# An fp32 encoder trunk on one core: split weights of the up projection 32 bytes off the line of the tokens, and one small load moved in the start

## The chip, the core and the metric

The kernel runs on one core of a Trainium2 chip (trn2). The metric is the device time of one execution in microseconds (us). The kernel before was timed in three runs: 2146.21, 2146.18 and 2145.07 us, median 2146.18. Names used below: TensorE is PE (its weight loads are listed apart as PEld), VectorE is DVE, ScalarE is ACT, GpSimd is POOL; SP only issues transfers (DMAs). SBUF is the on-chip memory of 128 partitions, PSUM the accumulation memory that PE writes.

## The reference

Two layers over 256 tokens of width 2048, everything in float32:

```
for l in range(2):
    h = rms_norm(x, ln1_g[l])
    qa, ka, va, qb, kb, vb = split(h @ w_in[l])           # 2048 -> 4608
    oa = neighborhood_attention(rms_norm(qa), rms_norm(ka), va, rpb[l])
    ob = windowed_gqa_sink(rope(rms_norm(qb)), rope(rms_norm(kb)), vb, sink[l])
    x = x + concat(rms_norm(oa), rms_norm(ob)) @ w_out[l]  # 2048 -> 2048
    h2 = rms_norm(x, ln2_g[l])
    u = depthwise_conv(h2 @ w_up[l], conv_w[l], conv_b[l]) # 2048 -> 11264
    gate, up = u[..., :5632], u[..., 5632:]
    x = x + (silu(gate) * up) @ w_down[l]                  # 5632 -> 2048
```

The weights are read once, 1 MB at a time; nearly all arithmetic is in the four projections.

## The kernel before

**Split products.** A float32 product is made from parts that PE takes at its faster format (float32r). Each operand is cut in two: a high part (ACT copies it rounded, line 103) and a low part (DVE subtracts the high part from the operand, line 104). For weights the parts are the tiles `whi` and `wlo`, 128 x 1024 each, made in `split_w` (lines 586 to 598) from a loaded tile `raw` (128 x 2048, 1 MB, two halves). For tokens the two parts lie side by side in one tile of 2 x 256 columns, called `xs` (the norm's output, 16 tiles, written in `prep_x`) or `mid` (attention's and the gate's outputs). Three of the four partial products are summed: high x high, low token x high weight, high token x low weight.

**Which operand moves.** A matmul has a stationary operand of 128 columns, which a weight load (PEld) brings into the array, and a moving operand that is streamed past it. In the input, output and down projections (`three`, line 387) the tokens are stationary and 512 columns of weights move. In the up projection (`two`, line 382) it is the other way round, so that the result stands transposed for the convolution:

```
mm(ps, w_h, mv, first, False)
mm(ps[:, 1], w_l, mv[:, 0], False, last)
```

The first of the two has a 128-column block of `whi` stationary and both halves of an `xs` tile moving, 512 columns. The second has the same block of `wlo` stationary and the 256 columns of the high half moving. A step of the up projection (half a `raw` tile) is eight such pairs, 16 matmuls; a feature block of 128 gate and 128 up columns is four steps, and there are 44 blocks in each of the two layers: 2 x 44 x 4 x 8 = 2816 pairs.

**The order of the work.** `quanta` (lines 550 to 571) lists the 1 MB pieces in order: 36 of the input projection, 16 of the output projection, and then, chunk by chunk, the up and the down projection. `steps` are their halves. The main loop (line 675) splits the weights four steps ahead (`SPLIT_AHEAD`), so `whi` and `wlo` have five buffers each; loads run three pieces ahead (`LOAD_AHEAD`) on SP's queue.

**Where tiles lie.** The constants come first in each partition of SBUF, then the pool of weights (`raw`, `whi`, `wlo`), then `mid`, `xs` and the rest. The tile `shift` (56 floats, line 73) holds no data and only takes room. In the built program `raw`, all five buffers of `whi` and of `wlo`, all 16 of `xs` and all 16 of `mid` begin 96 bytes past a multiple of 256; `x` begins 128 past one. A 128-column block is 512 bytes of a partition, an `xs` tile 2048, so every block, too, begins 96 past a multiple of 256. A tile `prob_a` of the attention begins 32 past one.

**The start.** ACT issues the load of the norm's weights `ln_g` (line 75) and of the first four pieces of `x` transposed (`mid<-in_xT`, line 605), SP the first 1 MB of weights in four parts, the next ones and the other pieces of `x`. `prep_x` (line 120) needs both a piece and `ln_g`. Eight semaphores, DMAHW0 to DMAHW7, are given to the DMAs in turn; a DMA that gets one in use waits, on its issuing engine, until the DMA before it on that semaphore has landed.

Of the kernel before, what the change touches and what calls it, by code (L numbers as in the profile page):

```python
# [12 lines left out]
F32R = mybir.dt.float32r  # L13
# [5 lines left out]
P = 128  # L19
# [13 lines left out]
FG = 4  # L33
CHUNKS = (12, 12, 12, 8)
# [8 lines left out]
SPLIT_AHEAD = 4  # L43
AHEAD_PRIO = 40
SHIFT = 56
WARM = 14


@with_exitstack
def encoder_kernel(  # L50
# [5 lines left out]
    nc = tc.nc  # L56
    const = ctx.enter_context(tc.tile_pool(name="const", bufs=1))
    wp = ctx.enter_context(tc.tile_pool(name="wp", bufs=2))
# [13 lines left out]

    const.tile([P, SHIFT], F32, name="shift")
    ln_g = const.tile([P, 2, L, KD], F32, name="ln_g")
    nc.scalar.dma_start(out=ln_g, in_=a["ln_g"])
    ident = const.tile([P, P], F32, name="ident")
    make_identity(nc, ident)
    ones = const.tile([P, P], F32, name="ones")
# [297 lines left out]
    quanta = []  # L376
# [28 lines left out]
    def q_win(l, j, u):  # L405
        def body(q, half, hi, lo):
            ps = banks("in", u == 0 and half == 0)
            hv, lv = (w.rearrange("p (k n) -> p k n", k=2) for w in (hi, lo))
            k = 4 * u + 2 * half
            three(ps, (xs[k], xs[k + 1]), hv, lv, k == 0, k == KD - 2)  # L410
            if half == 0:
                return
            if u == 0 and j == 0 and l > 0:
                load_qk_g(l)
            if u == 2 and j == 1:
                rope_tables(l)
            if u == 3:
                if l == 0 and j == 0:
                    at(q + 4, done_win, q, l, j, ps, half=0)
                else:  # L420
                    done_win(q, l, j, ps)
        return body
# [35 lines left out]
    def q_wout(l, grp, nb, u):  # L458
        def body(q, half, hi, lo):
            g = 0 if grp == "a" else 1  # L460
            ps = banks("out", u == 0 and half == 0)
            hv, lv = (w.rearrange("p (k n) -> p k n", k=2) for w in (hi, lo))
            h = 4 * u + 2 * half
            three(ps, (os[g * NH + h], os[g * NH + h + 1]), hv, lv, h == 0, h == NH - 2)
            if nb == 0 and u == 0 and half == 1:
                stat_o(grp)
            if u == 1 and half == 1:
                if grp == "b":
                    add_x(nb, ps, st["ro"])
                else:  # L470
                    whole_x(q, l, 1, nb, ps, st["ro"])
        return body
# [12 lines left out]
    def q_up(l, f, u):  # L485
        def body(q, half, hi, lo):
            if u == 0 and half == 0:
                cur["up"] = psum.tile([P, 2, 2, T], F32, name="mm", bufs=2)
            ps = cur["up"]
            hv, lv = (w.rearrange("p (k j n) -> p k j n", k=4, j=2) for w in (hi, lo))  # L490
            for j in range(2):
                for kk in range(4):
                    k = 8 * u + 4 * half + kk
                    two(ps[:, j], hv[:, kk, j], lv[:, kk, j], xs[k], k == 0, k == KD - 1)
            if u == 1 and half == 1:
                with tc.high_priority(offset=4 * AHEAD_PRIO if f == NF - 1 else 0):
                    glu(l, f, ps)
        return body
# [24 lines left out]
    def q_down(l, c, nb, g):  # L523
        f0, nf = sum(CHUNKS[:c]), CHUNKS[c]

        def body(q, half, hi, lo):
            ps = banks(("dn", nb), g == 0 and half == 0)
            hv, lv = (w.rearrange("p (k n) -> p k n", k=2) for w in (hi, lo))
            i = FG * g + 2 * half
            three(ps, (gs[f0 + i], gs[f0 + i + 1]), hv, lv, i == 0, i == nf - 2,  # L530
                  l == L - 1 and c == len(CHUNKS) - 1 and i == nf - 2)
            if g < nf // FG - 1 or half == 0:
                return
            if c < len(CHUNKS) - 1:
                add_x(nb, ps)
            elif l + 1 < L:
                whole_x(q, l + 1, 0, nb, ps)
            else:

                n = 2 if nb == NB - 1 else 1  # L540
                for tt in range(TT):
                    for i in range(n):
                        m = slice(i * 512 // n, (i + 1) * 512 // n)
                        xv = x[:, tt, nb * 512 + m.start:nb * 512 + m.stop]
                        nc.vector.tensor_add(xv, xv, ps[:, tt, m])  # L545
                        (nc.sync, nc.scalar)[i].dma_start(
                            out=out[:, tt, nb * 512 + m.start:nb * 512 + m.stop], in_=xv)
        return body

    for l in range(L):  # L550
        for j in range(NJ):
            for u in range(4):
                quanta.append((a["w_in"][l, j, u], q_win(l, j, u)))
        for grp in "ba":
            for nb in range(NB):
                for u in range(2):
                    quanta.append((a["w_out"][l, 0 if grp == "a" else 1, nb, u], q_wout(l, grp, nb, u)))
        f = 0
        for c, nf in enumerate(CHUNKS):

            end = min(sum(CHUNKS[:c + 1]) + 1, NF)
            while f < end:
                for u in range(2):
                    quanta.append((a["w_up"][l, f, u], q_up(l, f, u)))
                f += 1
            ng = nf // FG
            order = [(nb, g) for nb in range(NB) for g in range(ng)]
            if end == NF:
                order = sorted(order, key=lambda o: (o[0] // 2, o[1], o[0]) if o[0] < 2 else (1, 0, 0))
            for nb, g in order:  # L570
                quanta.append((a["w_down"][l, sum(CHUNKS[:c]) // FG + g, nb], q_down(l, c, nb, g)))


    steps = [(q, h) for q in range(len(quanta)) for h in range(2)]
# [1 line left out]
    raw, hl, left, loads, highs = {}, {}, {}, {}, {}  # L576
# [9 lines left out]
    def split_w(s, parts=1):  # L586
        if s < len(steps):
            q, half = steps[s]
            hl[s] = tuple(wp.tile([P, 1024], F32R, name=t, bufs=SPLIT_AHEAD + 1) for t in ("whi", "wlo"))
            m = 1024 // parts  # L590
            for j in range(parts):
                with tc.high_priority(offset=AHEAD_PRIO if s >= KD // 2 else 0):
                    highs[s] = split(*(t[:, j * m:(j + 1) * m] for t in hl[s]),
                                     raw[q][:, half * 1024 + j * m:half * 1024 + (j + 1) * m])
            left[q] -= 1
            if left[q] == 0:
                del raw[q]
                load(q + LOAD_AHEAD)
# [3 lines left out]
    for i in range(KD // 2):  # L602
        xT.append(act.tile([P, 2, T], F32, name="mid", bufs=16))
        if i < 4:
            nc.scalar.dma_start(out=xT[i], in_=a["xT"][:, 2 * i:2 * i + 2, :])
        if i == 1:

            nc.scalar.activation(const.tile([P, 1], F32, name="junk"), halfpi, AF.Copy)
# [156 lines left out]
```

## Time and profile before

| | us |
|---|---|
| median of three runs | 2146.18 |
| the profiled execution's own time | 2145.43 |
| its span, first to last instruction | 2143.6 |
| PE busy | 2135.3 |
| DVE busy | 1460.9 |
| ACT busy | 1141.2 |
| POOL busy | 66.5 |

The profile is of one execution. Its own time is 1.8 us longer than its span and 0.75 us shorter than the median. The granted clock of PE was 1.000 throughout, its upper level of 2.4 GHz. Matmuls are pipelined: the duration in a row is from the issue of one to the modelled end of its last column, so it is longer than the distance from one matmul's start to the next one's. The distances between starts are what adds up to the span.

### The profile page before, as it was taken

How to read it: one execution, taken by the hardware profiler on the slowest of the kernel's cores; microseconds unless marked ns; L12 is line 12 of the kernel's file. 1: busy time of each engine (PE TensorE's matmuls, PEld its weight loads, DVE VectorE, ACT ScalarE, POOL GpSimd, SP SyncE). 2: the span in 40 equal slices, each digit the busy share in tenths (PEclk: the TensorE clock that was granted, in tenths of full speed). 3: DMA queues.
4: the chain of work that ended last, by engine and by line, in shares of the span. 5: the costliest groups of instructions: out<-in, count | busy, mean ns of one | idle time of the engine just before them, and what ended most of it. 6: DMA issues, size and time to landing. Idle time of an engine off the chain costs nothing.

```text
span 2143.6 us, 28802 instructions
## 1 busy us (share of the span) xinstructions
PE 2135.3 (100%) x10904; PEld 1811.6 (85%) x10904; DVE 1460.9 (68%) x2293; ACT 1141.2 (53%) x1651; POOL 66.5 (3%) x215
## 2 busy tenths in 40 slices
PE   9999999999999999999999999999999999999999
PEld 7888888888888888888888888888888888888887
DVE  7777667775677567657756866677756775776575
ACT  6566556554455355535655665555545553554453
POOL 0000000000000000000000000000000000000000
PEclk9999999999999999999999999999999999999999
DMA  9544555555555555555555454555555555555553
GB/s 340 195 142 166 175 177 177 188 186 197 183 190 191 190 189 179 194 196 178 195 179 194 138 170 164 177 177 185 189 197 180 193 188 188 194 179 194 193 181 137
DMA packets 60844, 397.89 MB, mean 186 GB/s; under 512 B 7329, under 2 KB 9889, under 8 KB 13729
## 3 DMA queue, kind: packets, MB, share of 16 engines
q1 hardware_dynamic: 59696, 394.71, 54.0%
q8 instruction: 85, 1.39, 0.3%
q10 hardware_dynamic: 1008, 1.34, 0.2%
q14 instruction: 55, 0.44, 0.1%
HBM read 393.93 MB, written 2.10 MB: 185 GB/s over the span
## 4 chain that ended last, share of the span: by engine, by line
PE 99%; DMA 1%; ACT 0%; DVE 0%; issue 0%; DVEq 0%
PE mm L85 95%; PE pv L85 1%; PE S L85 1%; PE tr L291 1%; PE S L139 0%; DMA raw<-in_w_in 0%; PE tr L352 0%; PE tr L85 0%; ACT xs L106 0%; DMA ln_g<-in_ln_g 0%; ACT whi L103 0%; PE tr L347 0%; PE tr L344 0%; DVE x L545 0%; DVEq L760 0%
## 5 line engine op out<-in xcount | busy, mean ns | idle before, releaser
L104 DVE TENSOR_TENSOR wlo<-raw,whi 128x1024 fp32r<-128x1024 f32 (+1 forms) x737 | 901.2, 1223 | 560.0 <-ACT whi L103 520.4
L103 ACT ACTIVATE whi<-raw 128x1024 fp32r<-128x1024 f32 (+1 forms) x737 | 779.7, 1059 | 882.0 <-PE mm L85 680.2
L85 PE MATMUL mm<-xs,whi 128*128 128x512 f32 x2816 | 995.0, 399 | 0.0
L85 PE MATMUL mm<-xs,wlo 128*128 128x256 f32 x2816 | 790.9, 281 | 0.0
L85 PEld LDWEIGHTS mm<-xs,whi 128*128 128x128 f32 x2816 | 528.8, 188 | 131.3
L85 PEld LDWEIGHTS mm<-xs,wlo 128*128 128x128 f32 x2816 | 531.9, 189 | 0.7
L85 PE MATMUL mm<-whi,mid 128*128 128x512 f32 x1920 | 481.6, 391 | 0.0
L85 PEld LDWEIGHTS mm<-whi,mid 128*128 128x128 f32 x1920 | 357.9, 188 | 72.8
L85 PE MATMUL mm<-whi,xs 128*128 128x512 f32 x1152 | 296.1, 395 | 2.8 <-ACT whi L103 2.7
L85 PE MATMUL mm<-wlo,mid 128*128 128x512 f32 x960 | 260.0, 390 | 0.0
L85 PEld LDWEIGHTS mm<-whi,xs 128*128 128x128 f32 x1152 | 214.6, 188 | 47.4 <-ACT whi L103 3.4
L85 PEld LDWEIGHTS mm<-wlo,mid 128*128 128x128 f32 x960 | 180.1, 188 | 37.3
L85 PE MATMUL mm<-wlo,xs 128*128 128x512 f32 x576 | 162.0, 396 | 0.0
L516 DVE SCALAR_TENSOR_TENSOR pT<-halo,conv,pT 128x256 f32<-128x256 f32 x352 | 146.3, 474 | 0.2
L85 PEld LDWEIGHTS mm<-wlo,xs 128*128 128x128 f32 x576 | 107.3, 188 | 21.7 <-DVE wlo L104 0.4
L514 ACT ACTIVATE pT<-halo,conv 128x256 f32<-128x256 f32 x176 | 94.9, 587 | 0.1
L508 POOL COPY halo<-halo 128x6 f32<-128x6 f32 x88 | 18.5, 210 | 1453.9 <-DVE halo L506 1453.9
L506 DVE TENSOR_TENSOR halo<-prob,r 128x512 f32<-128x512 f32 x88 | 60.9, 692 | 2.7
L505 DVE TENSOR_TENSOR prob<-prob,mm 128x512 f32<-128x512 f32 x88 | 59.8, 680 | 0.0
L452 DVE TENSOR_TENSOR x<-x,mm 128x1024 f32<-128x1024 f32 x28 | 34.2, 1221 | 35.2 <-PE mm L85 35.2
L504 ACT ACTIVATE prob<-mm 128x512 f32<-128x512 f32 x88 | 51.0, 580 | 0.0
L519 DVE TENSOR_TENSOR prob<-prob,pT 128x256 f32<-128x256 f32 x88 | 36.8, 418 | 1.5 <-ACT prob L518 1.5
(129 smaller groups left out, 841.1 us busy)
## 6 DMA issues: line engine op xcount, KB each, us to landing
raw<-in_w_up SPq DMA_DIRECT2D x176, 1024.0 KB, 4.8
raw<-in_w_down SPq DMA_DIRECT2D x88, 1024.0 KB, 4.9
raw<-in_w_in SPq DMA_DIRECT2D x71, 1024.0 KB, 4.9
raw<-in_w_out SPq DMA_DIRECT2D x32, 1024.0 KB, 4.9
bias<-in_bias SPq DMA_DIRECT2D x16, 160.0 KB, 3.7
x<-in_x SPq DMA_DIRECT2D x4, 512.0 KB, 8.3
out<-x SPq DMA_DIRECT2D x6, 256.0 KB, 2.7
raw<-in_w_in SPq DMA_DIRECT2D x4, 256.0 KB, 5.7
```

The source lines that it names most:

```text
L85: nc.tensor.matmul(ps, lhsT, rhs, start=start, stop=stop, skip_group_check=True)
L103: high = nc.scalar.activation(hi, src, AF.Copy)
L104: nc.vector.tensor_sub(lo, src, hi.bitcast(F32))
L291: nc.tensor.transpose(ps[:, j, tt * P:(tt + 1) * P], qn[tt][:, p + j, :], ident)
L452: nc.vector.tensor_add(xv, xv, ps)
L504: nc.scalar.activation(t, ps[:, :, 0], AF.Copy)
L505: nc.vector.tensor_add(t, t, ps[:, :, 1])
L506: nc.vector.tensor_mul(ux[:, :, r:r + T], t, st["r2"][:, None, :].to_broadcast([P, 2, T]))
L508: nc.gpsimd.tensor_copy(ux[:, :, 1:r], ux[:, :, T:T + r - 1])
L514: nc.scalar.activation(y[:, j, :], ux[:, j, r:r + T], AF.Identity, scale=w1, bias=b)
L516: nc.vector.scalar_tensor_tensor(y[:, j, :], ux[:, j, o:o + T], w, y[:, j, :], op0=ALU.mult, op1=ALU.add)
L519: nc.vector.tensor_mul(t[:, 1, :], t[:, 0, :], y[:, 1, :])
```

## The change

There are two parts. First, `whi` and `wlo` get 64 floats (256 bytes) more per buffer, and a step of the up projection uses the 1024 columns from float 56 on, the others those from float 0 on. In the built program a step of the up projection then finds its split weights 64 bytes past a multiple of 256, that is 32 below its tokens (`xs`, still 96), and the other projections theirs at 96 as before. The buffers grow by 256 bytes each, so all that lies behind them moves up by 2560 bytes and keeps its place within 256. Second, the load of `ln_g` is issued behind that of the first piece of `x` and no longer ahead of it.

```
+UP_AT = 56
...
     ln_g = const.tile([P, 2, L, KD], F32, name="ln_g")
-    nc.scalar.dma_start(out=ln_g, in_=a["ln_g"])
...
-                    quanta.append((a["w_up"][l, f, u], q_up(l, f, u)))
+                    quanta.append((a["w_up"][l, f, u], q_up(l, f, u), True))
...
-            hl[s] = tuple(wp.tile([P, 1024], F32R, name=t, bufs=SPLIT_AHEAD + 1) for t in ("whi", "wlo"))
+            at_ = UP_AT if quanta[q][2] else 0
+            hl[s] = tuple(wp.tile([P, 1024 + 64], F32R, name=t, bufs=SPLIT_AHEAD + 1)[:, at_:at_ + 1024]
+                          for t in ("whi", "wlo"))
...
         if i < 4:
             nc.scalar.dma_start(out=xT[i], in_=a["xT"][:, 2 * i:2 * i + 2, :])
+        if i == 0:
+            nc.scalar.dma_start(out=ln_g, in_=a["ln_g"])
```

The pieces of the other three projections get `False` in the same place. The order of instructions on PE, DVE, POOL and SP is the same in both programs. It differs on ACT, at the head of its program; `mid_83` and `mid_82` below are the same first piece of `x`, `raw_97` the first 1 MB of weights, `xs0` and `xs1` the first two token tiles. Before:

```order
L75 DMA ln_g_72<-in_ln_g 128x64
L605 DMA mid_83<-in_xT 128x512
L605 DMA mid_85<-in_xT 128x512
L608 ACT_TABLE_LOAD
L608 ACTIVATE junk_87<-halfpi_81 128x1 [waits DVE_49]
L605 DMA mid_89<-in_xT 128x512
L605 DMA mid_91<-in_xT 128x512 [waits DMAHW1_49]
L106 ACTIVATE xs0_135<-mid_83,ln_g_72 128x256 [waits DMAHW3_49,DMAHW0_49]
L106 ACTIVATE xs1_138<-mid_83,ln_g_72 128x256
L103 ACTIVATE whi_141<-raw_97 128x512 [waits DMAHW2_49]
L103 ACTIVATE whi_141<-raw_97 128x512
```

The same head of ACT's program in the changed kernel:

```order
L608 DMA mid_82<-in_xT 128x512
L610 DMA ln_g_72<-in_ln_g 128x64
L608 DMA mid_85<-in_xT 128x512
L613 ACT_TABLE_LOAD
L613 ACTIVATE junk_87<-halfpi_80 128x1 [waits DVE_49]
L608 DMA mid_89<-in_xT 128x512
L608 DMA mid_91<-in_xT 128x512 [waits DMAHW1_49]
L107 ACTIVATE xs0_135<-mid_82,ln_g_72 128x256 [waits DMAHW3_49,DMAHW0_49]
L107 ACTIVATE xs1_138<-mid_82,ln_g_72 128x256
L104 ACTIVATE whi_141<-raw_97 128x512
L104 ACTIVATE whi_141<-raw_97 128x512 [waits DMAHW2_49]
```

The first two loads have changed places, and with them their semaphores: DMAHW0 was `ln_g`'s and is now the first piece's, DMAHW3 the other way round. The second 1 MB of weights, fifth DMA on SP, waits for DMAHW0 in both programs: before for the landing of `ln_g`, now for that of the first piece of `x`. The wait for DMAHW2 (the second quarter of the first weights) moved from the first to the second of the two halves of the first split.

## Rows read from the trace of the kernel before

**Rows 1.** The page's head, the busy time of PE, the granted clock of PE in 40 equal slices, and the chain of work that ended last, by engine and by line.

```profile
span 2143.6 us, 28802 instructions
...
PE 2135.3 (100%) x10904; PEld 1811.6 (85%) x10904; DVE 1460.9 (68%) x2293; ACT 1141.2 (53%) x1651; POOL 66.5 (3%) x215
...
PEclk9999999999999999999999999999999999999999
...
PE 99%; DMA 1%; ACT 0%; DVE 0%; issue 0%; DVEq 0%
```

**Rows 2.** The page's costliest groups: line, engine, operation, tiles and shapes, count, then busy us and mean ns of one, then idle us of the engine before them and what ended it.

```profile
L104 DVE TENSOR_TENSOR wlo<-raw,whi 128x1024 fp32r<-128x1024 f32 (+1 forms) x737 | 901.2, 1223 | 560.0 <-ACT whi L103 520.4
L103 ACT ACTIVATE whi<-raw 128x1024 fp32r<-128x1024 f32 (+1 forms) x737 | 779.7, 1059 | 882.0 <-PE mm L85 680.2
L85 PE MATMUL mm<-xs,whi 128*128 128x512 f32 x2816 | 995.0, 399 | 0.0
L85 PE MATMUL mm<-xs,wlo 128*128 128x256 f32 x2816 | 790.9, 281 | 0.0
...
L85 PEld LDWEIGHTS mm<-xs,wlo 128*128 128x128 f32 x2816 | 531.9, 189 | 0.7
```

**Rows 3.** PE's timeline from 405 us on, inside the up projection of the first layer: start us, duration us, engine, line, operation, tiles, shape, count. 98 pairs lie between the first row's start and the last row's.

```profile
404.77 0.40 PE L85 MATMUL mm<-xs,whi 128*128 128x512 f32 x1
405.00 0.28 PE L85 MATMUL mm<-xs,wlo 128*128 128x256 f32 x1
405.12 0.40 PE L85 MATMUL mm<-xs,whi 128*128 128x512 f32 x1
405.35 0.28 PE L85 MATMUL mm<-xs,wlo 128*128 128x256 f32 x1
405.47 0.40 PE L85 MATMUL mm<-xs,whi 128*128 128x512 f32 x1
405.71 0.28 PE L85 MATMUL mm<-xs,wlo 128*128 128x256 f32 x1
405.83 0.40 PE L85 MATMUL mm<-xs,whi 128*128 128x512 f32 x1
...
439.39 0.40 PE L85 MATMUL mm<-xs,whi 128*128 128x512 f32 x1
```

**Rows 4.** PE's timeline from 485 us on, inside the down projection of the first layer; rows of the same tiles are merged with their count, the first number is the start of the first.

```profile
487.06 1.07 PE L85 MATMUL mm<-wlo,mid 128*128 128x512 f32 x4
487.96 1.98 PE L85 MATMUL mm<-whi,mid 128*128 128x512 f32 x8
489.78 1.07 PE L85 MATMUL mm<-wlo,mid 128*128 128x512 f32 x4
```

**Rows 5.** PE's timeline from 340 us on, at the very beginning of the up projection of the first layer. Nine pairs lie between the first row's start and the last row's.

```profile
340.48 0.39 PE L85 MATMUL mm<-xs,whi 128*128 128x512 f32 x1
340.71 0.28 PE L85 MATMUL mm<-xs,wlo 128*128 128x256 f32 x1
340.82 0.39 PE L85 MATMUL mm<-xs,whi 128*128 128x512 f32 x1
...
343.60 0.39 PE L85 MATMUL mm<-xs,whi 128*128 128x512 f32 x1
```

**Rows 6.** PE's timeline at two places where a 512-column matmul of the projections is followed by a transpose of the attention, whose stationary block begins elsewhere within 256 bytes. The weight load (PEld) of the transpose begins with the matmul ahead of it.

```profile
224.43 0.14 PEld L344 LDWEIGHTS tr<-ident,prob_a 128*128 128x128 f32 x1
224.67 0.27 PE L344 MATMUL tr<-ident,prob_a 128*128 128x128 f32 x1
...
147.24 0.39 PE L85 MATMUL mm<-wlo,xs 128*128 128x512 f32 x1
147.47 0.38 PE L352 MATMUL tr<-ident,prob 128*128 128x128 f32 x2
```

**Rows 7.** Busy us of each engine, with counts, in a stretch inside the up projection (us from the span's start), then the granted clock, the DMA share and GB/s. The columns are PE, PEld, DVE, ACT, POOL.

```profile
360.00:480.00 120.00, 120.00 (x681) 104.09 (x680) 90.98 (x131) 67.05 (x97) 6.42 (x22) 1.00 0.55 189
```

**Rows 8.** The chain that ended last, in order of time, over the first 25 us: start us, us, what.

```profile
0.73 3.68 DMA ln_g<-in_ln_g
...
4.43 8.43 DMA raw<-in_w_in
...
12.88 2.01 ACT whi L103 x2
14.89 3.27 ACT xs L106 x9
...
19.89 2.11 PE mm L85 x8
```

**Rows 9.** The timeline of the start: the two DMA issues on ACT's queue, ACT's first token tile with the idle time before it, and PE's first matmul of a projection.

```profile
0.73 0.41 ACTq L75 DMA_DIRECT2D ln_g<-in_ln_g  x1
...
1.17 0.94 ACTq L605 DMA_DIRECT2D mid<-in_xT  x2
...
6.60 0.91 ACT L106 ACTIVATE xs<-mid,ln_g 128x256 fp32r<-128x256 f32 x2 [2.96 <-DMA mid<-in_xT]
...
8.54 0.91 ACT L106 ACTIVATE xs<-mid,ln_g 128x256 fp32r<-128x256 f32 x2
```

**Rows 10.** The page's DMA issues: what, queue, count, KB each, median us from issue to landing.

```profile
raw<-in_w_in SPq DMA_DIRECT2D x71, 1024.0 KB, 4.9
```

More of the change, by code (lines that the diff above doesn't have):

```diff
@@ L552, in encoder_kernel @@
             for u in range(4):
-                quanta.append((a["w_in"][l, j, u], q_win(l, j, u)))
+                quanta.append((a["w_in"][l, j, u], q_win(l, j, u), False))
         for grp in "ba":
@@ L556, in encoder_kernel @@
                 for u in range(2):
-                    quanta.append((a["w_out"][l, 0 if grp == "a" else 1, nb, u], q_wout(l, grp, nb, u)))
+                    quanta.append((a["w_out"][l, 0 if grp == "a" else 1, nb, u], q_wout(l, grp, nb, u), False))
         f = 0
@@ L570, in encoder_kernel @@
             for nb, g in order:
-                quanta.append((a["w_down"][l, sum(CHUNKS[:c]) // FG + g, nb], q_down(l, c, nb, g)))
+                quanta.append((a["w_down"][l, sum(CHUNKS[:c]) // FG + g, nb], q_down(l, c, nb, g), False))
     steps = [(q, h) for q in range(len(quanta)) for h in range(2)]
```

## The prediction

> **What bounds the kernel now.** I read the page's head and its chain first: PE is busy for 2135.3 of 2143.6 us, the chain that ended last is 99% PE, and the clock stands at its upper level in every slice [rows 1]. So the time is the sum of the distances from one matmul's start to the next, and an edit counts by what it does to those distances. Then the groups: the up projection is 2816 pairs of a 512-column and a 256-column matmul, each with a weight load of its own, and PE stood idle before none of them [rows 2]. DVE and ACT, which split the weights, were idle for 560 and 882 us before their splits, ACT mostly because it waited for PE to free a buffer [rows 2]; in 120 us of the up projection they are busy for 91 and 67 us [rows 7]. They follow PE and do not set the pace.
>
> The durations of rows 2 can't be used for the price, as they overlap. The timeline gives the distances. In the up projection 98 pairs take from 404.77 to 439.39 us, 34.62 us, or 353.3 ns a pair [rows 3]. Times 2816 that is 995 us, 46% of the execution. In the down projection twelve matmuls of 512 columns take from 487.06 to 489.78, or 226.7 ns each [rows 4]. If the 512-column matmul of the up projection took no more, the other one would be left with 126.6 ns; the rows show 0.23 to 0.24 us for the first and 0.12 for the second [rows 3]. So the same 512 columns cost some 10 ns more here than there, though both have one weight load beside them and both read blocks that lie alike within 256 bytes.
>
> One more thing in the timeline decides what I forecast. The distances are not constant in time. Deep in the up projection the 512-column matmul alternates between 0.23 and 0.24 us [rows 3]; at its beginning, with the same tiles and the same shapes, nine pairs take from 340.48 to 343.60, 3.12 us, or 346.7 ns each, steadily [rows 5]. Nothing waited in either stretch. The same work thus has two paces, and what differs can only be how the two streams that PE reads, the moving columns and the next stationary block, lie to each other in time. The part of the change that counts shifts just that: where the one stream begins in memory beside the other.
>
> **The change part by part.**
>
> *Offset of the split weights.* It adds no instruction and no wait. Per pair both weight loads now read from 32 bytes below the line of the moving tokens. The trace before has no load at that offset in this projection, so its cost is bounded from both sides:
>
> - From below by the shortest distance of either matmul that the rows show with a load beside it: 226.7 ns [rows 4] and 0.11 us (340.71 to 340.82) [rows 5], together 337 ns. That is 16.3 ns less than now, times 2816: 46 us off.
> - From above by the longest pair in the rows, 405.47 to 405.83, 0.36 us, taken by every pair and not by one in three [rows 3]: 6.7 ns more, times 2816: 19 us on top. A farther end: the load of a transpose's block that lies 64 bytes below the line of the moving weights. From its start to the transpose is 224.43 to 224.67, 0.24 us [rows 6], where a load in line takes 226.7 ns [rows 4]; 13 ns more on each 512-column matmul would be 37 us on top. With the block 96 bytes above the line it was 0.23 (147.24 to 147.47) [rows 6].
>
> I take the value that the same work has already shown, the steady pace at the beginning of the up projection: 353.3 - 346.7 = 6.6 ns a pair, times 2816 pairs = 18.6 us off. It is nearest to the rows (same tiles, same shapes, same loads), and it lies between the two ends.
>
> The Trainium skill speaks against any effect: SBUF — State Buffer, section "Who interferes with whom", gives PE two read ports, one for the moving operand and one for weight loads, which are independent of each other. By that rule the offset changes nothing and the sum is zero. The trace doesn't bear it out as it stands: two paces for the same work [rows 3, 5] are hard to explain without some dependence between the two streams. The page TensorE: Matmul & The Clock Gate, section "Back-to-back issue gap", gives N / 2.4 + 2.5 ns for a lone matmul, an estimate of 216 + 109 = 325 ns a pair, which would be 80 us off; no row here shows so short a pair.
>
> *Writes to the shifted tiles.* In 352 steps (2816 pairs, eight to a step) one write of ACT and one of DVE go 32 bytes elsewhere. ACT takes 1059 ns and DVE 1223 for one [rows 2], and a step of eight pairs lasts 2.83 us. Even if each took a fifth longer, DVE's share in rows 7 would rise from 91 to about 102 of 120 us. Cost nothing; the cover is the idle time of both engines. The larger buffers add no wait.
>
> *The load of `ln_g` behind the first piece of `x`.* The start is bound by transfers: PE's steady work begins at 19.89 us, behind ACT's splits, which run without a pause from 12.88, when the second 1 MB of weights has landed [rows 8]. That load was issued at 4.43, the moment `ln_g` had landed. Now it waits for the first piece of `x`. This one was issued at 1.17 and ACT began to use it at 6.60, 5.4 us later [rows 9]; issued at 0.73 it would land about 6.1. So the weights' load goes out some 1.7 us later, and behind it on SP's queue wait the other pieces of `x`. The load took 8.43 us [rows 8], where one of the same size takes 4.9 later on [rows 10]: 3.5 us of it were spent behind transfers issued earlier. A start 1.7 us later fits into that, as the same bytes are ahead of it. I cost it at nothing, with the ends -0.4 us (the first piece comes 0.44 us sooner, and all follows) and +1.7 us (nothing is absorbed). The first matmuls may start 0.4 us sooner, but ACT's next tile already stands at 8.54 behind the first ones [rows 9], and all of them meet again at the landing at 12.85.
>
> **Sum.** The profiled execution took 2145.4 us. 2145.4 - 18.6 + 0 = 2126.8. The median of the runs is 0.75 us above the profiled execution: 2127.6, which I round to 2127.
>
> **The rivals.**
>
> 1. *The offset does nothing.* The two streams don't depend on the offset, and the two paces have another cause, such as the moment at which a stretch begins. For it: the profile names no wait, and all blocks of rows 3 and 5 lie alike, so within the rows it is not the address that makes the difference. Against it: so far no other cause is in sight. Time 2146, give or take the 1.7 us of the start. The rule of the skill's SBUF page would give this time.
> 2. *Slower: the offset moves every load into the worse of the places that the streams can have.* The pairs of rows 3 change between 0.35 and 0.36 us; the alternation shows that a part of them meets a better place by itself, as each pair's length moves the next. A fixed offset can hold all of them at the bad one: +19 us, 2165; with the 13 ns of rows 6 on each 512-column matmul 2183. It decides as soon as the mean pair is above 353.3 ns. For it: a block 64 bytes below the line gave the longest distance of rows 6, and 32 bytes below lies between that and the line. Against it: that was a transpose's load, which is another kind of instruction (0.14 us against 0.19).
> 3. *Faster by much more:* both matmuls reach their shortest distances, 337 ns a pair, 46 us off, 2100. For it: the down projection holds 226.7 ns over its whole length [rows 4]. Against it: in the up projection no pair does.
>
> **How the numbers follow.** Forecast, a pair near 347 ns, with the cases around it down to 340: 0.50. Rival 3: 0.08. Rival 1: 0.18. Rival 2: 0.24. A measurement of this kernel can tell a difference of about 0.2%, 4.3 us, from none. Faster by more than that: 0.50 + 0.08 = 0.58. Within it: 0.18. Slower: 0.24. The likeliest case's own range is 2106 to 2139 us (pairs of 339 to 351 ns). The range for 8 in 10 reaches from 2100, the lower bound, to 2162: it takes in rival 1 and about half of rival 2, and leaves out some 0.05 below and 0.13 above.
>
> **What would show it.** In the profile after, the starts in PE's timeline inside the up projection: 98 pairs in 34.0 us or less if I am right, 34.6 for rival 1, 35 or more for rival 2, 33.0 for rival 3. The pace should be steady and no longer alternate. The distances in the input, output and down projections should stay at 226.7 ns. In the start, the second weights' load should be issued near 6.1 us and still land within 0.5 us of 12.85; if PE's steady work begins past 21, that step is wrong. The forecast as a whole is wrong if the mean pair stays above 351 ns.

## The result and the profile after

| | before | after |
|---|---|---|
| median of the runs beside each other, us | 2145.62 (2144.95 to 2146.21, four runs) | 2126.09 (2125.99 to 2126.18, four runs) |
| ratio | | 0.9909, 95% interval 0.9892 to 0.9926 |
| the profiled execution's own time, us | 2145.43 | 2126.1 |

The changed kernel is 0.9% faster, about 19.5 us. The forecast was 2127, its range 2100 to 2162.

The head of the page after, with the busy time, the granted clock in 40 slices and the chain that ended last, answers to [rows 1]:

```profile
span 2124.3 us, 28802 instructions
...
PE 2118.1 (100%) x10904; PEld 1815.3 (85%) x10904; DVE 1458.0 (69%) x2293; ACT 1141.2 (54%) x1651; POOL 142.1 (7%) x215
...
PEclk9999999999999999999999999999999999999999
...
PE 99%; DMA 0%; ACT 0%; DVE 0%; ACTq 0%; DVEq 0%; issue 0%
```

The number of instructions is the same, PE is still the bound and the clock at its upper level. The whole gain is in PE's busy time, 2135.3 to 2118.1, and the 2 us around it. POOL's busy time doubled, which nobody asked for; the last section comes back to it.

The costliest groups after (busy us, mean ns of one, idle us of the engine before them) answer to [rows 2]. Lines 104 to 107 of the changed kernel are lines 103 to 106 of the one before, line 86 was 85:

```profile
L86 PE MATMUL mm<-xs,whi 128*128 128x512 f32 x2816 | 976.6, 390 | 0.0
L105 DVE TENSOR_TENSOR wlo<-raw,whi 128x1024 fp32r<-128x1024 f32 (+1 forms) x737 | 901.2, 1223 | 543.8 <-ACT whi L104 504.9
...
L86 PE MATMUL mm<-xs,wlo 128*128 128x256 f32 x2816 | 794.1, 282 | 0.0
```

The 512-column matmul of the up projection became 9 ns shorter (399 to 390), the 256-column one did not. These durations overlap, so the price is read from the starts. PE's timeline from 405 us on (start us, duration us) answers to [rows 3]:

```profile
404.82 0.39 PE L86 MATMUL mm<-xs,whi 128*128 128x512 f32 x1
405.05 0.28 PE L86 MATMUL mm<-xs,wlo 128*128 128x256 f32 x1
405.17 0.39 PE L86 MATMUL mm<-xs,whi 128*128 128x512 f32 x1
405.39 0.28 PE L86 MATMUL mm<-xs,wlo 128*128 128x256 f32 x1
405.51 0.39 PE L86 MATMUL mm<-xs,whi 128*128 128x512 f32 x1
...
438.79 0.39 PE L86 MATMUL mm<-xs,whi 128*128 128x512 f32 x1
```

Between the first and the last row lie 98 pairs, as in [rows 3], in 33.97 us: 346.6 ns a pair, where it was 34.62 us and 353.3. A pair is now always 0.34 or 0.35 us and no longer 0.35 and 0.36. In the trace as a whole the pairs away from other work average 346.67 ns. The down projection beside it (timeline from 484 us on, rows of the same tiles merged, answers to [rows 4]):

```profile
484.45 1.98 PE L86 MATMUL mm<-whi,mid 128*128 128x512 f32 x8
486.27 1.07 PE L86 MATMUL mm<-wlo,mid 128*128 128x512 f32 x4
487.17 1.98 PE L86 MATMUL mm<-whi,mid 128*128 128x512 f32 x8
```

Twelve matmuls in 487.17 - 484.45 = 2.72 us, 226.7 ns each, as before. So (353.3 - 346.67) x 2816 = 18.7 us of the difference between the two profiled executions, 19.3 us, come from the pace of the up projection. The rest is the start. Its chain in order of time (start us, us, what) answers to [rows 8]:

```profile
1.17 5.02 DMA ln_g<-in_ln_g
...
6.28 0.91 ACT xs L107 x2
7.19 0.53 ACT whi L104
...
7.76 0.50 PE mm L86
...
8.28 12.82 PE mm L86 x55
```

And the timeline of the start, by ACT and by SP's queue, answers to [rows 9]:

```profile
6.28 0.91 ACT L107 ACTIVATE xs<-mid,ln_g 128x256 fp32r<-128x256 f32 x2 [2.64 <-DMA ln_g<-in_ln_g]
...
11.98 2.01 ACT L104 ACTIVATE whi<-raw 128x1024 fp32r<-128x1024 f32 x2 [1.21 <-DMA raw<-in_w_in]
```

```profile
0.73 4.41 SPq L585 DMA_DIRECT2D raw<-in_w_in  x5
```

Before, PE's first matmul of a projection, which the text of [rows 9] names and its rows don't show, was this one:

```profile
8.59 2.11 PE L85 MATMUL mm<-whi,xs 128*128 128x512 f32 x8 [2.69 <-ACT whi L103]
```

Now `ln_g`, issued second, is what ACT waits for, the first projection matmul starts at 7.76 instead of 8.59, and the second 1 MB of weights has landed at 11.98, not 12.88. The fifth issue of SP's row is that load; the row ends at 0.73 + 4.41 = 5.14 us.

### The profile page after: what moved, and what is told of

It is laid out like the page before. It is cut to its first block, busy times and chain, and to the rows that moved or that the text cites. A ratio compares the mean times of both kernels' runs of the same rounds, so it can differ in the third digit from the quotient of the medians.

```text
span 2124.3 us, 28802 instructions
## 1 busy us (share of the span) xinstructions
PE 2118.1 (100%) x10904; PEld 1815.3 (85%) x10904; DVE 1458.0 (69%) x2293; ACT 1141.2 (54%) x1651; POOL 142.1 (7%) x215
## 4 chain that ended last, share of the span: by engine, by line
PE 99%; DMA 0%; ACT 0%; DVE 0%; ACTq 0%; DVEq 0%; issue 0%
PE mm L86 95%; PE pv L86 1%; PE S L86 1%; PE tr L292 1%; PE S L140 0%; PE tr L353 0%; PE tr L86 0%; DMA ln_g<-in_ln_g 0%; PE tr L348 0%; PE tr L345 0%; DVE x L546 0%; ACT xs L107 0%; ACT whi L104 0%; ACTq L608 0%; DVEq L765 0%
## 5 line engine op out<-in xcount | busy, mean ns | idle before, releaser
L105 DVE TENSOR_TENSOR wlo<-raw,whi 128x1024 fp32r<-128x1024 f32 (+1 forms) x737 | 901.2, 1223 | 543.8 <-ACT whi L104 504.9
L86 PE MATMUL mm<-xs,whi 128*128 128x512 f32 x2816 | 976.6, 390 | 0.0
L509 POOL COPY halo<-halo 128x6 f32<-128x6 f32 x88 | 22.7, 258 | 1359.8 <-DVE halo L507 1359.8
L510 POOL COPY halo<-halo 128x6 f32<-128x6 f32 x88 | 95.1, 1081 | 0.2 <-POOL halo L509 0.2
```

What stands on the lines that cost most here:

```text
L86: nc.tensor.matmul(ps, lhsT, rhs, start=start, stop=stop, skip_group_check=True)
L105: nc.vector.tensor_sub(lo, src, hi.bitcast(F32))
L509: nc.gpsimd.tensor_copy(ux[:, :, 1:r], ux[:, :, T:T + r - 1])
L510: nc.gpsimd.tensor_copy(ux[:, :, T + r:T + 2 * r - 1], ux[:, :, r + 1:2 * r])
```

## The experiments

The theory: the time of a pair depends on where the stationary blocks begin beside the moving tokens, modulo 256 bytes, and on nothing else of the change. Offsets below are given as weights minus tokens, modulo 256; the change is 224. A pace is the mean distance from the start of one high-part matmul to the next in the trace; where a block of 32 pairs has an offset of its own, its first 14 pairs are left out. The first block of each layer has matmuls of other work between its pairs, and its pace is less certain.

**One part at a time.** The changed kernel with `ln_g` loaded first again (offset alone), and with `UP_AT = 0` (the moved load and the larger buffers alone):

```
+    nc.scalar.dma_start(out=ln_g, in_=a["ln_g"])
...
-        if i == 0:
-            nc.scalar.dma_start(out=ln_g, in_=a["ln_g"])
```

> The changed kernel with the load of the norm's weights back in its old place, ahead of the first piece of x: only the offset of 32 bytes in the up projection is left. Theory A (the offset makes the whole pace of the up projection, 346.7 ns a pair): about 18.4 us below the kernel before, near 2127, and PE's first matmul of a projection again near 8.6 us. If the 0.9 us that the start of the changed kernel gained came from a chance of that run and not from the moved load, the start may come out either way here.

> The changed kernel with an offset of 0: the larger weight buffers and the moved load stay. Theory A: the up projection is back at 353.3 ns a pair, so the time is within 1 us of the kernel before, some 0.9 us below it if the moved load is what brought the start forward (first projection matmul near 7.8 us, second weights landed near 12.0), and equal if not. Rival (the larger buffers, not the offset, changed the pace): about 18 us below.

| | us | ratio to before |
|---|---|---|
| offset alone | 2126.50 (5 runs) | 0.9915 (0.9902 to 0.9929) |
| moved load and larger buffers alone | 2144.77 (11 runs) | 0.9998 (0.9990 to 1.0007) |
| before, beside both | 2144.93 (15 runs) | |

The offset is the change. The moved load is worth nothing that these timed runs can tell. The second kernel also bears out that offsets count modulo 256: its split weights lie in buffers an odd multiple of 256 bytes apart, and its pairs took 353.2 ns on average, as before. The groups of the second kernel have the up projection back at the durations of [rows 2]:

```profile
L86 PE MATMUL mm<-xs,whi 128*128 128x512 f32 x2816 | 995.0, 399 | 0.0
```

**Other offsets.** One kernel gives each five feature blocks of the up projection another offset; one does so with the input and down projections, whose tokens are stationary and whose weights move (the output projection stays in line there).

```
-                    quanta.append((a["w_up"][l, f, u], q_up(l, f, u), True))
+                    quanta.append((a["w_up"][l, f, u], q_up(l, f, u), UP_STEPS[l][f // 5]))
...
-            at_ = UP_AT if quanta[q][2] else 0
+            at_ = quanta[q][2]
```

> The changed kernel with the offset of the up projection's weights set anew for every five feature blocks: in the first layer 0, 32, 64, 96, 128, 160, 192, 224 bytes and 0 again, in the second 16, 48, 80, 112, 144, 176, 208, 240 and 224. Theory A (the offset between the two streams sets the pace): each offset has a pace of its own, 353.3 ns a pair at 0 both times, 346.7 at 224 bytes. Rival (either pace can hold at any offset, by how a stretch begins): 353.3 and 346.7 turn up without order, and the two stretches at 0, or the stretch at 224, differ from the whole kernels. I expect paces between 340 and 365.

> The changed kernel, up projection as it is, with the moving weights of the input projection (one offset per job) and of the down projection (one per five pieces) set to the same series of offsets. In line these matmuls take 226.7 ns each. Theory A: the distance changes with the offset here too, and in line need not be the best; I expect 220 to 240 ns. If it stays at 226.7 at all offsets, the dependence is one of the up projection alone.

The mean distances by offset; those of the down projection, where no other work lies between the matmuls, by the offset of its stationary tokens from the moving weights:

```
offset, bytes      0          16    32    48    64    80    96   112   128   144   160   176   192   208   224         240
up pair, ns    353.0       346.9 353.3 346.7 353.2 353.2 346.7 353.3 351.1 349.3 350.0 349.3 353.3 349.9 346.7 346.7/353.3
down mm, ns    226.7 226.7/236.5 233.3 234.7 233.4 233.3 234.2 233.3 233.2 226.7 233.3 231.2 229.0 233.3 233.4       231.8
```

The first took 2136.78 us, the second 2143.91, one run each. Two numbers stand where stretches at one offset differ: the up projection at 240 held 346.7 ns in the two blocks ahead of a stretch of the down projection and 353.3 in the three behind it; the down projection at 16 took 236.5 in one piece and 226.7 in the four of the next stretch. So the theory's "each offset has a pace of its own" already fails at these places. Each kind of matmul has its own list of good offsets: nothing is better than in line for the down projection (144 equals it), and in line is among the worst for the up projection, where 16, 48, 96 and 224 reach 346.7 to 346.9. Nothing grows steadily with the distance: for the up projection 32 bytes above the tokens (32) is no better than in line, 32 below (224) is among the best. In the input projection, in the two jobs of each layer that no other work disturbs, the matmuls took, by the same offset of tokens from weights, 233.4 ns at 224, 233.3 at 208, 229.0 at 192 and 231.2 at 176, as in the down projection.

**Offset or address.** The kernel before with its up projection's tokens moved up by 32 bytes, the weights where they were; and with `SHIFT` 48 for 56, so that everything lies 32 bytes lower and stays in line.

```
-        xs[k] = act.tile([P, 2, T], F32R, name=f"xs{k}")
+        at_ = XS_AT if which == 1 else 0
+        xs[k] = act.tile([P, 2 * T + 64], F32R, name=f"xs{k}")[:, at_:at_ + 2 * T].rearrange("p (j t) -> p j t", j=2)
```

> The kernel before, with the split tokens of the up projection moved up by 32 bytes (128 past a multiple of 256) and the weights left at 96: again the weights begin 32 below the tokens, but at their old address. Theory A (the offset between the two streams counts): 346.7 ns a pair, about 18 us below the kernel before. Rival B (the address of the weights counts, 64 past a multiple of 256): 353.3 ns and the time of before.

> The kernel before, with the placeholder tile 32 bytes shorter, so that weights and tokens all begin at 64 past a multiple of 256, still in line. Theory A: nothing changes, 353.3 ns a pair and the time of before. Rival B (the address of the weights counts): 346.7 ns and about 18 us below.

Tokens moved: 2127.31 us (two runs), ratio 0.9917 (0.9888 to 0.9945). All moved: 2145.87 (eight runs), ratio 1.0001 (0.9990 to 1.0013). The weights' address is the old one in the first, and the weights' address is the change's in the second. So it is the relative offset that counts. Past the first block of the up projection ACT and DVE write `whi` and `wlo` and read `raw`, while `xs` is read by PE alone; that moving `xs` by itself gives the pace of the change shows that the two operands of PE count, and not how its weights lie to the tiles of other engines.

**Two paces at one offset.** Before each feature block but the first a small extra matmul, of 16 to 128 columns, shifts the moment at which the block is entered; layer 0 has offset 0, layer 1 has 224.

```
+                if f:
+                    kick = psum.tile([P, T], F32, name="pv", bufs=1)
+                    mm(kick[:, 0:16 * (f % 8) + 16], ones, ones[:, 0:16 * (f % 8) + 16], True, True)
```

> The changed kernel with offset 0 in the first layer and 32 below in the second, and ahead of each feature block but the first of a layer one small extra matmul of 16 to 128 columns whose result is not used, to throw the matmuls out of step. Theory A in its strict form (the offset alone sets the pace): the first layer's blocks fall back to 353.3 ns a pair within some ten pairs, the second layer's to 346.7. Theory C (at offset 0 both paces can hold, and the way a stretch begins decides, as at the beginning of the up projection in the kernel before): some blocks of the first layer run at 346.7 to their end, others at 353.3; in the second all run at 346.7.

It took 2153.07 us, with 86 matmuls more. At offset 224 every block ran at 346.6 to 346.7 ns. At offset 0 eight of the 43 blocks behind an extra matmul (2, 6, 10, 16, 22, 30, 34 and 40) held 346.5 ns to their end, the other 35 ran at 352.9 to 353.6. PE's timeline in blocks 1 and 2, 18 pairs from the first row to the last in each fence:

```profile
350.87 0.40 PE L86 MATMUL mm<-xs,whi 128*128 128x512 f32 x1
...
357.23 0.40 PE L86 MATMUL mm<-xs,whi 128*128 128x512 f32 x1
```

```profile
362.33 0.40 PE L86 MATMUL mm<-xs,whi 128*128 128x512 f32 x1
...
368.57 0.40 PE L86 MATMUL mm<-xs,whi 128*128 128x512 f32 x1
```

6.36 and 6.24 us, 353.3 and 346.7 ns a pair: the same tiles, shapes and offset, in neighbouring blocks. An offset can thus hold more than one pace, as Theory C had it; the strict form of Theory A is wrong. Between such blocks nothing differs but how they are entered. What in the entry decides was not found: the width of the extra matmul alone doesn't, as 48 columns led to 346.5 ns in blocks 2, 10 and 34 and to 353.5 in 18, 26 and 42. What [rows 3] and [rows 5] showed side by side is this.

**Finer steps.** The up projection's weights in steps of 4 bytes, a block each, and the same for each 1 MB piece of the down projection.

```
+                    quanta.append((a["w_up"][l, f, u], q_up(l, f, u), (NF * l + f) % 64))
```

> The changed kernel with another offset of the up projection's weights for each feature block, in steps of 4 bytes: 0 to 252 bytes, and from the 65th block on 0 to 92 again. Theory A: the pace is a function of the offset, the blocks with the same offset agree, and 353.3 ns at 0 and 346.7 at 224 come out as in the whole kernels. I expect that no offset goes below 346 ns; one that does would be a better kernel.

> The up projection keeps its offset; in the down projection each 1 MB piece has its own offset of the split weights from the tokens, 0 to 252 bytes in steps of 4. Theory (a pair or a lone matmul has a floor that depends only on which streams run side by side, and an offset can only reach it or miss it): no offset of the down projection is below 226.7 ns a matmul, several reach it, others lie up to 10 ns above; mean about 231, that is 1408 x 2 x 4.5 ns = some 10 to 15 us over the changed kernel, near 2138. Rival (the floor of 226.7 is the price of one place, a finer offset gives less): at some offsets a distance of 224 ns or less.

The up projection (2136.77 us, one run): 16 of the 64 offsets (16, 24, 44, 48, 84, 96, 152, 164, 180, 184, 196, 204, 224, 232, 240 and 244) reach 346.4 to 346.8 in every block that has them; 0 and 8 did so in one of their two blocks. Of the 24 offsets that occur twice, 0, 8 and 20 differ by more than 1 ns between their blocks (at 20 it is 353.7 and 350.1); the others agree. No offset is below 346. Two are far above the rest: 156 with 361.6 and 60 with 364.2 and 364.4. PE's timeline at 60 bytes:

```profile
572.64 0.39 PE L85 MATMUL mm<-xs,whi 128*128 128x512 f32 x1
572.87 0.28 PE L85 MATMUL mm<-xs,wlo 128*128 128x256 f32 x1
572.99 0.40 PE L85 MATMUL mm<-xs,whi 128*128 128x512 f32 x1
573.23 0.28 PE L85 MATMUL mm<-xs,wlo 128*128 128x256 f32 x1
573.34 0.42 PE L85 MATMUL mm<-xs,whi 128*128 128x512 f32 x1
573.60 0.29 PE L85 MATMUL mm<-xs,wlo 128*128 128x256 f32 x1
573.74 0.39 PE L85 MATMUL mm<-xs,whi 128*128 128x512 f32 x1
...
579.20 0.39 PE L85 MATMUL mm<-xs,whi 128*128 128x512 f32 x1
```

Here the pairs take 0.35, 0.35 and 0.40 us in turn, 18 of them 6.56 us. The same work over all 2816 pairs would be (364.3 - 353.3) x 2816 = 31 us slower than before; that whole kernel wasn't run. The down projection (2140.09 us, one run; offsets again as stationary minus moving, here tokens minus weights) found no offset below the 226.7 ns of in line; the next best was 228.4 at 196, the worst some 240 at 60, 156, 188 and 236. At 144, which had held 226.7 in the coarse sweep, it was some 231 here: two paces again. The theory's floor held; that several offsets reach it did not, as only in line did. Its time came near for a wrong reason: it counted 2816 matmuls at some 231 ns, where the down projection has 2112 (1056 in each layer) and they averaged some 233.5. 2112 x 6.8 ns is 14 us, and the run was 14.0 us above the changed kernel.

**Two offsets.** The high and the low part get offsets of their own, all 64 combinations of multiples of 32 bytes, a block each.

```
-            hl[s] = tuple(wp.tile([P, 1024 + 64], F32R, name=t, bufs=SPLIT_AHEAD + 1)[:, at_:at_ + 1024]
-                          for t in ("whi", "wlo"))
+            at_ = quanta[q][2]
+            hl[s] = tuple(wp.tile([P, 1024 + 64], F32R, name=t, bufs=SPLIT_AHEAD + 1)[:, o:o + 1024]
+                          for t, o in (("whi", at_ % 64), ("wlo", at_ // 64)))
```

> The high and the low split weights of the up projection get offsets of their own, all 64 combinations of multiples of 32 bytes, a block each. Theory (each weight load meets the moving stream of the matmul it lies beside, so each of the two has an offset of its own that counts): pairs between 346.7 and 356 ns, the good ones 346.7, with the price of the high and of the low part adding up; none below 346.7. Rival (only one of the two loads matters): the pace follows the one offset and is the same for all values of the other. Rival (346.7 is no floor): a combination near 342 or less, which would make a faster kernel than the changed one.

It took 2134.54 us. The pace in ns by the offset of the high part (across) and of the low part (down); the first 24 combinations occur in both layers, with two numbers where they differ by over 0.3. The first number at 0 and 0 and the one at high 128, low 160 are from the disturbed first blocks of the layers:

```
low\high      0           32          64          96          128    160    192         224
  0     349.7/353.3     351.3   349.9/353.1 346.8/349.9     352.1  349.3  340.2/350.1 344.4/346.7
 32        346.7        353.4      351.1       343.5        352.1  349.4     346.6       348.8
 64        346.8     351.3/348.4   353.2       348.4        346.7  348.9     346.7       346.7
 96        346.6        353.3      353.4       346.7        351.8  353.3     348.9       346.6
128        346.7        353.2      350.1       351.2        351.4  346.6     346.6       348.9
160        350.9        350.7      353.3       353.4        351.1  350.0     349.2       353.3
192        351.2        351.2      353.3       353.3        353.3  353.6     353.4       353.3
224        353.0        346.5      350.9       346.8        346.7  346.6     349.0       346.7
```

Both offsets count, so the rival by which only one load matters falls; but they don't add up, which the theory had said: the high part at 32 for 0 costs 6.7 ns with the low part at 96 and nothing with it at 160 or 192. And 346.7 is no floor. High 192 and low 0 gave 340.2 in one block and 350.1 in the other, again two paces at one place; high 96 and low 32 gave 343.4 and 343.5.

**A faster kernel.** First a look at whether these hold: in layer 0 22 blocks at 96 and 32 and 22 at 192 and 0, in layer 1 44 combinations around them.

> In layer 0 the up projection's first 22 blocks have the high split weights 96 bytes above the line of the tokens and the low ones 32 above, the other 22 blocks 192 and 0; in layer 1 each block has a combination of its own: high 80, 88, 96, 104, 112, 176, 184, 192, 200, 208 or 224, low 0, 16, 32 or 48. Theory (the pace is a function of the two offsets, and at some of them of how a block is entered): the first 22 blocks hold 343.5 ns a pair throughout, as two single blocks of the run before did; in the second 22 some blocks hold 340.2 and some 350.1 ns, as the two single blocks did; time near 2134. Rival (the two short paces were an accident of how those blocks were entered, and 346.7 is the floor): both halves settle at 346.7 or above. In layer 1 the theory leaves open whether a combination stays below 343; one that does would make the fastest kernel.

2123.25 us. Behind its first block, which other work disturbs (352.1), the first half held 343.3 ns in all 21 blocks; the second half held 340.0 in all 22, also in the two stretches that are entered from the down projection. The theory's guess that some of them would be at 350 was wrong, the rival's 346.7 too. In layer 1 the same 192 and 0, in a single block, ran at 350.0. No combination there was below 340; high 192 with low 16 came to 340.0 and high 88 with low 0 to 340.8, each in a single block. So the last kernel enters 192 and 0 only from a down projection's stretch, and uses 96 and 32 up to there:

```
+    def up_at(l, f):
+        return 24 + 64 * 8 if f < 13 else 48
```

(24 and 8 floats are 96 and 32 bytes, 48 and 0 are 192 and 0.)

> In both layers the up projection's first 13 blocks have the high split weights 96 bytes and the low ones 32 bytes above the line of the tokens, the other 31 blocks 192 and 0, which they enter from a down projection's stretch. Theory (the pace follows the two offsets, and a stretch entered from the down projection holds 340.0 ns at 192 and 0): 2 x 13 x 32 = 832 pairs of 343.3 ns and 1984 of 340.0, against 346.67 in the changed kernel: 2.8 + 13.2 = 16.0 us less than its 2126.1, so 2110.1 us. Rival (the other stretches lock at 350.1 ns, as single blocks did): 832 x 3.3 = 2.8 us less and 1984 x 3.4 = 6.8 us more, 2130.

2110.77 us (2110.44 to 2110.98, five runs), ratio to before 0.9839 (0.9825 to 0.9852): 15.3 us faster than the changed kernel, where the theory gave 16.0. Its groups and PE's timeline deep in layer 0, 18 pairs from the first row to the last:

```profile
L85 PE MATMUL mm<-xs,whi 128*128 128x512 f32 x2816 | 961.2, 389 | 0.0
L85 PE MATMUL mm<-xs,wlo 128*128 128x256 f32 x2816 | 779.7, 277 | 0.0
```

```profile
623.88 0.39 PE L85 MATMUL mm<-xs,whi 128*128 128x512 f32 x1
624.11 0.28 PE L85 MATMUL mm<-xs,wlo 128*128 128x256 f32 x1
624.22 0.39 PE L85 MATMUL mm<-xs,whi 128*128 128x512 f32 x1
624.45 0.28 PE L85 MATMUL mm<-xs,wlo 128*128 128x256 f32 x1
...
630.00 0.39 PE L85 MATMUL mm<-xs,whi 128*128 128x512 f32 x1
```

6.12 us, 340.0 ns a pair. In the blocks at 192 and 0 the wide matmul takes 226.7 ns on average and the narrow one 113.3, half of it. All 62 blocks at 192 and 0 ran at 339.9 to 340.1.

## Why the prediction was right, and where not

*PE is the bound, and the distances are the sum.* Right. The gain in the up projection came out at the end of the program undiminished: 18.7 of 19.3 us, and the last kernel's time followed its pairs as well (16.0 us expected, 15.3 measured). The sum of 2126.8 us for the profiled execution compares with 2126.1; the 0.75 us added for the median did not recur, as the median after was 2126.09, and the 2127.6 was rounded down to 2127.

*The steady pace at the beginning of the up projection is what the offset will hold.* The size was right to 0.1 us (18.6 and 18.7), and so was the reading that one kind of work has two paces with no wait in either: the extra matmuls show that directly. That the two streams' places in time are what differs stays a reading; the runs show that their offset in memory counts, and how a stretch is entered. [rows 5] isn't the very beginning of the up projection, though. Its first twelve pairs took 338.54 - 334.30 = 4.24 us, 353.3 ns each, and only behind eight transposes for the norm (`S<-ident,x`) that came between the pairs did the pace become 346.7:

```profile
334.30 0.39 PE L85 MATMUL mm<-xs,whi 128*128 128x512 f32 x1
...
338.54 0.40 PE L85 MATMUL mm<-xs,whi 128*128 128x512 f32 x1
338.77 0.38 PE L139 MATMUL S<-ident,x 128*128 128x128 f32 x2
...
339.34 0.82 PE L139 MATMUL S<-ident,x 128*128 128x128 f32 x6
```

The kernel before thus held a case of what the extra matmuls showed later: a small piece of other work between the pairs, and another pace behind it. And nothing in the argument pointed to 32 bytes below rather than to another place. Only 16 of the 64 offsets of the fine sweep reached that pace in all their blocks (one of them, 240, did not hold it in the coarse sweep), about two thirds were below 351.8 ns, a gain of 4.3 us or more, and the mean over all was some 350.5 ns ((2136.77 - 2126.09) / 2816 = 3.8 ns above 346.7), which would have been 8 us off and not 18.6. The step took a pace that the rows had shown for the pace that this offset would give; that it was this one is a hit among several places and not a result of the working.

*The rule that speaks against it.* The Trainium skill, SBUF — State Buffer, section "Who interferes with whom", has PE's two read ports independent of each other. The runs contradict this for the pairs measured here: 32 bytes between the operands, with shapes, counts and clock the same, are worth 6.6 ns a pair, and weights 60 bytes above the tokens cost 11 in the two blocks that had them. That the two reads meet somewhere in the memory is the simplest reading, but no run looked inside; what is shown is that the pace follows the relative offset and the way a stretch is entered. The prediction's estimate of 325 ns a pair, from the Trainium skill, TensorE: Matmul & The Clock Gate, section "Back-to-back issue gap", wasn't reached at any offset; the shortest settled pace was 340.0.

*Writes to the shifted tiles cost nothing.* Right: DVE took 1223 ns a subtract, as before, and its share of 120 us in the up projection, in the same window as [rows 7], is as it was:

```profile
360.00:480.00 120.00, 120.00 (x693) 106.34 (x692) 90.96 (x132) 68.92 (x98) 14.88 (x22) 1.00 0.55 188
```

PE got 693 matmuls into it and not 681.

*The load of `ln_g` behind the first piece of `x` costs nothing.* The size was right, the mechanism wrong. I took the 5.4 us from the issue of the first piece of `x` to ACT's use of it for that load's own time, and let the second weights' load wait until 6.1. It went out by 5.1 at the latest, so the piece of `x`, now issued first, had landed by then. In these traces the 5 us belong to whichever load is issued second: `x` with `ln_g` ahead of it (1.17 to 6.42 in the kernel with the offset alone), `ln_g` with `x` ahead of it (1.17 to 6.19). The weights did not land within 0.5 us of 12.85 but at 11.98. Their load went out some 0.4 us later than before (4.43 before; now about 4.8, as SP's row of five ends at 5.14 and one issue takes 0.33) and still landed 0.9 sooner, after some 7.2 us for 8.43; why it took less isn't shown. PE's matmul number 400, counted from 0, started at 93.36 us before and at 92.49 after. That is 0.9 us less, below the lower end of -0.4 that I had given; between the kernels that differ in nothing else it is 0.4 and 0.6 us (92.92 to 92.49, 93.36 to 92.80). One profile each is thin for that, as kernels with the same start differ too: the four with the old order of the two loads have this matmul at 92.87 to 94.01, the nine with the new order and an unchanged input projection at 92.34 to 92.80. So the new order does start sooner, by some 0.7 us on average, and in the timed runs it is nothing that can be told.

*The rivals.* "The offset does nothing" fell with the kernel of the offset alone. "Slower" is no error as a mechanism: offsets of 60 and 156 bytes hold a worse pace than in line. The transposes' load of [rows 6] was no guide to which: 64 bytes below the line (192) the up projection held 353.3 ns, as in line, and not 13 ns more. "Faster by much more" fell for one common offset; with an offset for each part it comes near, 340.0 against its bound of 337.

## What to carry to other kernels

When matmuls run back to back and the profile names no wait, compare the distances between starts, not the durations, and look for one shape that runs at two paces: it says that something other than the work sets the pace. Where such a pair reads two operands at once, their place beside each other is a free parameter, to be swept a block at a time in one kernel, separately for each operand, since the good places can't be told from the code. Before a pace is relied on, see whether it holds for whole stretches and however they are entered: a single block can show a pace, good or bad, that the next one doesn't have.

## What was not expected of the hardware

**Some paces recur.** Many stretches settle at a mean pair of 340.0, 343.3, 346.7, 350.0 or 353.3 ns, some 3.3 ns apart, and keep to it. It is no rule: five blocks in a row held 351.1 at an offset of 128 bytes and 349.3 at 144, and 60 and 156 bytes gave 364 and 362. At 340.0 the wide matmul has the down projection's 226.7 ns for 512 columns, and the narrow one half of that for 256.

**POOL's small copy.** POOL's busy time went from 66.5 to 142.1 us, and 71.5 of these 75.6 us are one instruction, the second of two 128 x 6 copies of the convolution's edge. It is in the groups of the kernel before, and of the one after:

```profile
L509 POOL COPY halo<-halo 128x6 f32<-128x6 f32 x88 | 23.6, 268 | 0.2 <-POOL halo L508 0.2
```

```profile
L510 POOL COPY halo<-halo 128x6 f32<-128x6 f32 x88 | 95.1, 1081 | 0.2 <-POOL halo L509 0.2
```

The timelines of POOL and of DVE at the same place of the program, before and then after, show why:

```profile
563.07 0.19 POOL L509 COPY halo<-halo 128x6 f32<-128x6 f32 x1
...
563.10 1.23 DVE L104 TENSOR_TENSOR wlo<-raw,whi 128x1024 fp32r<-128x1024 f32 x1 [0.28 <-ACT whi L103]
```

```profile
559.37 1.25 POOL L510 COPY halo<-halo 128x6 f32<-128x6 f32 x1
...
559.34 1.23 DVE L105 TENSOR_TENSOR wlo<-raw,whi 128x1024 fp32r<-128x1024 f32 x1 [0.23 <-ACT whi L104]
```

Before, the copy began 0.03 us ahead of DVE's subtract and took 0.19 us. After, it begins 0.03 us behind it and ends at 560.62, when the subtract has ended at 560.57. The same holds for all copies of this line after: 74 of the 88 started well inside a subtract, and each of them ended 46 to 49 ns behind it; the other 14 took under 0.2 us. The Trainium skill, SBUF — State Buffer, section "Who interferes with whom", has a DVE instruction with two SBUF inputs contend with a GpSimd instruction that reads SBUF, over a shared pair of ports that it calls an exclusive lock. The trace agrees. It costs nothing here, as the trace shows no one waiting for these copies.
